# Listing an expert layer's tokens in one burst of bf16 products, and adding up a paired expert earlier

## The chip, the cores and the metric

The kernel runs on one core of one Trainium2 chip. The metric is device microseconds of one execution, from the first to the last instruction of the program with what lies around them. A core has a matrix engine (TensorE, PE in the profile, with its weight loads shown apart as PEld), a vector engine (VectorE, DVE), a scalar engine (ScalarE, ACT), a general engine (GpSimd, POOL) and a queue engine that here only issues transfers (SyncE, SP). Weights come from HBM over 16 DMA engines.

## The reference, cut to what matters

Two transformer layers over 256 tokens of width 1024. The second layer ends in a mixture of experts: each token goes to 2 of 8 experts, and this part reads most of the bytes, since every expert has three matrices of 1024 x 3584 float32 (44 MB).

```python
logits = (xf @ router).astype(jnp.float32)
top_v, top_i = lax.top_k(logits, TOP_K)
gates = jax.nn.softmax(top_v, axis=-1)
dense_g = jnp.sum(jax.nn.one_hot(top_i, N_EXPERTS) * gates[..., None], axis=1)
y = jnp.zeros_like(xf)
for e in range(N_EXPERTS):
    y = y + dense_g[:, e:e + 1] * swiglu(xf, wg[e], wu[e], wd[e])
# swiglu(x, wg, wu, wd) = (silu(x @ wg) * (x @ wu)) @ wd
```

All inputs and the output are float32. After it comes a residual layer norm.

## The kernel before, in words

The attention parts and the dense channel mixer of the first layer take the first third of the time; the change does not touch them. `Route` finds, for each token and expert, whether the token is chosen (`maskf`), its place in the expert's list (`pos`) and its weight (`gate`). `Route.ones` issues small products whose results nobody uses, between the two halves of the router's products.

The experts run in the order `ORDER = [1, 0, 2, 4, 5, 6, 7, 3]`; below, position 0 is expert 1, and so on. Each is entered through a `tc.Switch` on the number of its tokens, with one arm for each of six sizes (`CLASSES`). In the profiled data position 0 and position 4 take the same arm, `(64, 0)`: up to 64 tokens, two column groups of the array side by side. Positions 1 and 2 (`HEAVY` and `LIGHT`) run as a pair, group by group in turns, in `both()`: the heavy one has up to 128 tokens in split precision (three products each, from parts `wh` and `wl` that ScalarE and VectorE write) and a second part of 32 tokens ("beyond"); the light one has 32.

An expert's columns are cut into two chunks, c = 0 (2048 columns) and c = 1 (1536). Its stages are: gate products (m = 0) and up products (m = 1) for c = 0, the same for c = 1, then the down products for both chunks. Weights move in pieces of 1 MB (42 to an expert) through 18 buffers (`halves`). `done(u)` issues the transfer of the piece 18 places later on SP's queue as soon as a piece has been used. So TensorE can be up to 18 pieces behind the transfers, and the transfers stop where all 18 are full.

Tokens of an expert are fetched by `gather`: GpSimd clears `x_sb` and issues an indirect transfer from the rows `x_rows` in HBM, at the row numbers `slot_row`. They are then transposed on TensorE and copied (`pick`), into `xg`. `bring` adds an expert's result to the sum `acc`: four products with a one-hot matrix, then four VectorE additions.

`list_tokens` makes `slot_row`. For each of eight experts VectorE writes a one-hot matrix of 2 x 256 columns in float32 (L978), into halves of one tile, so that two experts fit at a time; TensorE multiplies it with the token numbers in four products of one column each (L981); at the end VectorE turns the sums into row numbers (L982, L983). A float32 product is two weight loads and two matmuls in the trace. The call stands ahead of the c = 1 chunk of position 0:

```python
if i == 0 and c == cs[-1]:
    list_tokens()
    gather(HEAVY, 0)
    gather(LIGHT, 0, 32, 1)
```

At the end of the pair, `bring_light` (`before_end`) is called after the heavy expert's last group of down products. Then the "beyond" part is added up (`scatter_few`, L1193 and L1196, over two "tr" and two "mm" banks of PSUM), the next expert's tokens are picked through two "mm" banks (one copy on VectorE, one on ScalarE, L1184), and the heavy expert is brought in (L1010, L1014). PSUM has 8 banks here: four "acc", two "mm" and two "tr".

The code gives an order, from which a planner makes each engine's instruction list ahead of the run. It may move an instruction forward into a gap that it foresees. [...]

Of the kernel before, what the change touches and what calls it, by code (L numbers as in the profile page):

```python
# [194 lines left out]
def body(ctx, nc, tc, a, out, n_experts=E):  # L195
# [39 lines left out]
    with tc.tile_pool(name="split", bufs=4, side="right") as sp, \  # L235
# [580 lines left out]
        for t in range(2):  # L816
            route.logits(t, ps_tr, ps_mm, x_sb, ident)
            route.choose(t)
            if t == 0:
                route.ones(ps_acc, 20)  # L820
        route.places(ps_tr)
        route.both(ORDER[HEAVY], ORDER[LIGHT])
        gate.close()
# [5 lines left out]
def moe(ctx, nc, tc, a, out, raws, x_sb, hd, route, ident, neghalf, psums, dram, n_experts):  # L829
# [31 lines left out]
    def abreast(m, c):  # L861
        return 4 if m < 2 and c == 0 else 2
# [93 lines left out]
    def whole(tag, n=1024, pool_=wk):  # L956
        return pool_.tile([P, n], F32, name=tag)
# [9 lines left out]
    slot_row = mc.tile([P, 2 * E], I32, name="slot_row")  # L967
    NONE = 2.0 * S

    def list_tokens():  # L970

        tok = whole("wh", pool_=sp)
        pool.iota(tok[:, :2], pattern=[[P, 2]], base=-int(NONE), channel_multiplier=1, allow_small_or_imprecise_dtypes=True)
        ohs, tp = whole("wh", pool_=sp), bank("tr")
        for i, e in enumerate(ORDER[:n_experts]):
            o = ohs[:, i % 2 * 2 * S:(i % 2 + 1) * 2 * S].rearrange("p (t n) -> p t n", t=2)
            for t in range(2):
                dve.tensor_scalar(o[:, t], iota, pos[:, t, e:e + 1], route.maskf[:, t, e:e + 1], op0=ALU.is_equal, op1=ALU.mult)  # L978
            for h in range(2):
                for t in range(2):  # L980
                    pe.matmul(tp[:, 2 * i + h:2 * i + h + 1], o[:, t, h * P:(h + 1) * P], tok[:, t:t + 1], start=t == 0, stop=t == 1)  # L981
        dve.tensor_scalar(slot_token, tp[:, :2 * E], NONE, None, op0=ALU.add)  # L982
        dve.tensor_copy(slot_row, slot_token)  # L983

    def gather(i, h, n=P, to=None):
# [195 lines left out]
    def pick(q, kind="tr"):  # L1181

        tp = picked(x_sb, oh, 4 * q) if kind == "tr" else gathered(0, P, 4 * q, 4, kind)
        (act.copy if q else dve.tensor_copy)(xg[:, q * 512:(q + 1) * 512], tp)  # L1184

    def scatter_few(sc, y):

# [17 lines left out]
    def expert(i, cls, mine, sc2, after=None, before_end=None, mate=None):  # L1205
        e, ws = ORDER[i], widths(i)
        final = i + 1 == n_experts
        parts = [mate] if mate else [Part(xg, *p_) for p_ in CLASSES[cls]]
        paired = mate or before_end
        grouped = final and parts[0].n == 32  # L1210
# [17 lines left out]
        turn = parts[:]  # L1228
        cs = ds = range(len(ws))

        def by_turns(units, n, f, between=None):

            for u0 in range(0, len(units), n):
                yield
                for p_ in turn:
                    if p_ in to_pick:
                        to_pick.remove(p_)
                        pick_beyond(p_)
                    for u in units[u0:u0 + n]:
                        f(p_, u)  # L1240
                turn.reverse()
                for u in units[u0:u0 + n]:
                    done(u)
                if between:
                    between(u0 + n)

        def down(c):
            units = units_of(i, c, 2)

            def between(n):  # L1250

                if c == ds[-2]:
                    for p_ in parts:
                        p_.turned(ws[-1], {1: {4: (0, 1), 6: (2,)}, 2: {4: (0,), 6: (1,)}, 4: {6: (0,)}}[p_.g].get(n, ()))


            narrow = {1: 4, 3: 1, 5: 3}.get(cls, 0)
            yield from by_turns(units, abreast(2, c) if paired else len(parts), lambda p_, u: p_.down(
                u, c == 0 and u[3] == 0, c == ds[-1] and u == units[-1],
                256 if c == ds[-1] and u[3] < narrow and not p_.off else 512), between)  # L1260

        for c in cs:
            width = ws[c]
            if i == 0 and c == cs[-1]:
                list_tokens()
                gather(HEAVY, 0)
                gather(LIGHT, 0, 32, 1)
            if beyond and c == cs[-1]:
                shares(sc2, e, P, beyond[0].n)
            for m in range(2):  # L1270

                n = abreast(m, c) if paired else 4 if few and c < cs[-1] else len(parts)
                units = units_of(i, c, m)
                turn[:] = parts if len(units) // n % 2 else parts[::-1]
                if m == 0 and c == cs[0]:
                    turn[:] = parts
                yield from by_turns(units, n, lambda p_, u: p_.products(m, u))
                if m == 0 and c > cs[0] and not at_once:
                    for p_ in parts:
                        p_.turned(ws[c - 1])  # L1280
                for p_ in turn[::-1]:
                    p_.active(m, width)
            if at_once and c < cs[-1]:
                for p_ in parts:
                    p_.turned(width)
# [20 lines left out]
        turn[:] = parts[::-1]  # L1306
        if before_end:
            gather(i + 2, 0)
        yield from down(len(ws) - 1)
        if before_end:  # L1310
            before_end()
        for p_ in beyond:
            if few and not final:
                act.copy(p_.h[0][:, :S], p_.y[0][:, :S])
# [115 lines left out]
    for i, e in enumerate(ORDER):  # L1430
        if i == LIGHT:
            continue
        if i == 0:
            onehot(oh, e, 0, route.maskf)
            for q in range(2):
                pick(q)
            for t in range(2):
                act.activation(acc[:, t], x_sb[:, t], AF.Copy, scale=ALPHA)
            arms[HEAVY] = (nc.values_load(route.pair[0:1, 0:1], min_val=0, max_val=len(HEAVY_ARMS) - 1), len(HEAVY_ARMS))
        else:  # L1440
            for q in range(2):
                pick(q, "mm")
            bring(sc, ORDER[i - 2 if i - 1 == LIGHT else i - 1])
            if i != HEAVY and i + 1 < n_experts:
                gather(i + 1, 0)
        for cls in tc.Switch(*arms[i], f"expert{i}"):
            if i != HEAVY:
                run(expert(i, cls, sc, sc2, i + 1))
            elif cls:
                both()  # L1450
            else:

                gather(LIGHT, 0)
                flow, usual = laid(False), (flow, place)
                place = {u: q for q, u in enumerate(flow)}
                for q in range(len(halves)):
                    fetch(pair_start + q)
                for q in range(2):
                    pick(q, "mm")
                gather(HEAVY, 0)  # L1460
                for kind in tc.Switch(kinds[ORDER[LIGHT]], len(CLASSES), "light"):
                    run(expert(LIGHT, kind, sc, sc2))
                for q in range(2):
                    pick(q, "mm")
                bring(sc, ORDER[LIGHT])
                gather(LIGHT + 1, 0)
                for kind in tc.Switch(kinds[ORDER[HEAVY]], len(CLASSES), "heavy"):
                    run(expert(HEAVY, kind, sc, sc2, LIGHT + 1))
                flow, place = usual
# [14 lines left out]
```

## Time and profile before

| what | value |
|---|---|
| runs | 1330.01 us median of 3 (1320.58 to 1333.2) |
| profiled execution | 1327.82 us, of which 1326.0 us from the first to the last instruction |
| mean granted TensorE clock | 0.97 |
| TensorE busy | 1267.2 us (96%) |
| VectorE, ScalarE, GpSimd busy | 459.3, 360.9, 45.3 us |
| moved from HBM | 427.73 MB |

The profile is of one execution. Times of a row are in microseconds from the span's start, or lengths; a group's mean is in nanoseconds. "idle before <-X" names what the engine waited for. A matmul's length in a row includes the time that its result takes to come out, so in a row of many the union of all, not the sum, is the time spent. "PEclk" is the share of full clock that TensorE was granted.

### The profile page before, as it was taken

What the parts mean: (1) busy time and instruction counts of PE and PEld (TensorE: products, weight loads), DVE (VectorE), ACT (ScalarE), POOL (GpSimd) and SP (SyncE); (2) the same over time, 40 slices, a digit from 0 to 9 for tenths busy, and PEclk for the clock granted to TensorE, in tenths of its full rate; (3) what the DMA queues carried; (4) which work ended last, traced back from release to release, by engine and by line L of the source; (5) the groups of instructions that cost most, each with busy time, mean ns of one, the idle gap of its engine ahead of it and who ended that gap; (6) DMA issues with size and microseconds to landing.
All of it is one profiled execution on the core that took longest, in us unless ns stands there. A gap on an engine that the chain in (4) does not pass through costs nothing.

```text
span 1326.0 us, 21614 instructions
## 1 busy us (share of the span) xinstructions
PE 1267.2 (96%) x8971; PEld 777.5 (59%) x8971; DVE 459.3 (35%) x742; ACT 360.9 (27%) x638; POOL 45.3 (3%) x64
## 2 busy tenths in 40 slices
PE   9999999999998799999999999999999999999974
PEld 8978999998987454545665642443542443243331
DVE  4689455567677210336544440001010001000102
ACT  4584444453573100244543410000000000000001
POOL 1010000000001000000000000000000000000000
PEclk9999999999999889999999999999999999999985
DMA  9537455553627899989999979998999999999895
GB/s 331 203 96 258 187 190 182 178 205 136 219 96 302 312 417 406 395 363 410 408 420 418 420 297 377 361 367 330 415 418 415 413 419 415 388 420 412 337 417 241
DMA packets 98026, 430.60 MB, mean 325 GB/s; under 512 B 10403, under 2 KB 16547, under 8 KB 67244
## 3 DMA queue, kind: packets, MB, share of 16 engines
q1 hardware_dynamic: 95804, 422.75, 80.9%
q0 software_dynamic: 2032, 5.63, 1.3%
q8 instruction: 81, 1.33, 0.4%
q14 instruction: 109, 0.89, 0.2%
HBM read 427.73 MB, written 2.11 MB: 324 GB/s over the span
## 4 chain that ended last, share of the span: by engine, by line
PE 82%; DMA 6%; issue 2%; DVE 2%; ACT 1%; POOL 0%; SPq 0%; DVEq 0%; ACTq 0%; POOLq 0%
PE acc L1090 15%; PE acc L1153 15%; PE mm L1090 14%; PE mm L344 4%; PE mm L343 4%; PE mm L345 4%; PE acc L1023 3%; PE acc L345 3%; PE acc L1025 3%; PE acc L344 3%; PE acc L343 3%; PE acc L1024 3%; DMA piece<-in_moe_w_down_dram 3%; PE tr L1123 2%; DMA piece<-in_moe_w_up_dram 1%
## 5 line engine op out<-in xcount | busy, mean ns | idle before, releaser
L1090 PE MATMUL acc<-piece,xg 128*64 128x512 f32 (+5 forms) x1488 | 191.9, 502 | 0.0
L1153 PE MATMUL acc<-piece,hT 128*32 128x256 f32 (+2 forms) x1504 | 175.2, 459 | 8.9 <-DMA piece<-in_moe_w_down_dram 8.9
L307 DVE TENSOR_TENSOR wl<-piece,wh 128x1024 fp32r<-128x1024 f32 (+4 forms) x124 | 135.0, 1098 | 87.9 <-ACT wh L305 85.1
L1090 PE MATMUL mm<-piece,xg 128*64 128x512 f32 (+5 forms) x896 | 143.2, 528 | 15.1 <-issue 5.5
L305 ACT ACTIVATE wh<-piece 128x1024 fp32r<-128x1024 f32 (+4 forms) x124 | 118.1, 958 | 81.6 <-PE acc L344 40.6
L1090 PEld LDWEIGHTS acc<-piece,xg 128*32 128x32 f32 (+1 forms) x1488 | 71.4, 120 | 114.6 <-issue 101.1
L1153 PEld LDWEIGHTS acc<-piece,hT 128*32 128x32 f32 (+1 forms) x1504 | 71.0, 123 | 104.2 <-issue 72.2
L343 PE MATMUL mm<-xTh,wl 128*128 128x256 f32 x448 | 126.7, 283 | 0.0
L344 PE MATMUL mm<-xTh,wh 128*128 128x256 f32 x448 | 126.5, 282 | 0.0
L345 PE MATMUL mm<-xTl,wh 128*128 128x256 f32 x448 | 126.4, 282 | 0.0
L1104 DVE TENSOR_TENSOR hd<-hd,acc 128x512 f32<-128x512 f32 (+1 forms) x24 | 14.5, 630 | 298.7 <-PE acc L1090 297.2
L838 DVE TENSOR_TENSOR wl<-piece,wh 128x1024 fp32r<-128x1024 f32 (+1 forms) x80 | 88.1, 1117 | 76.2 <-PE acc L1025 51.0
L1090 PEld LDWEIGHTS mm<-piece,xg 128*64 128x64 f32 (+1 forms) x896 | 56.9, 131 | 96.2 <-issue 84.7
L1111 ACT ACTIVATE hT<-tr 128x512 f32<-128x512 f32 (+2 forms) x30 | 15.6, 542 | 327.9 <-PE tr L1123 315.2
L837 ACT ACTIVATE wh<-piece 128x1024 fp32r<-128x1024 f32 (+1 forms) x80 | 75.8, 973 | 68.8 <-PE acc L1024 68.6
L343 PEld LDWEIGHTS mm<-xTh,wl 128*128 128x128 f32 x448 | 85.0, 190 | 0.2
L344 PEld LDWEIGHTS mm<-xTh,wh 128*128 128x128 f32 x448 | 84.2, 188 | 0.2
L345 PEld LDWEIGHTS mm<-xTl,wh 128*128 128x128 f32 x448 | 84.2, 188 | 0.0
L1169 DVE COPY hd<-acc 32x256 f32<-32x256 f32 (+2 forms) x12 | 6.6, 554 | 163.4 <-ACT hd L1169 107.5
L343 PE MATMUL acc<-wh,xTl 128*128 128x512 f32 (+2 forms) x128 | 46.7, 365 | 0.0
L345 PE MATMUL acc<-wl,xTh 128*128 128x512 f32 (+2 forms) x128 | 46.3, 363 | 0.0
L344 PE MATMUL acc<-wh,xTh 128*128 128x512 f32 (+2 forms) x128 | 46.2, 361 | 0.0
(474 smaller groups left out, 1648.2 us busy)
## 6 DMA issues: line engine op xcount, KB each, us to landing
piece<-in_moe_w_down_dram SPq DMA_DIRECT2D x95, 1024.0 KB, 15.5
piece<-in_moe_w_gate_dram SPq DMA_DIRECT2D x60, 1024.0 KB, 14.1
piece<-in_moe_w_up_dram SPq DMA_DIRECT2D x58, 1024.0 KB, 16.2
piece<-in_moe_w_up_dram SPq DMA_DIRECT2D x30, 768.0 KB, 10.2
piece<-in_moe_w_gate_dram SPq DMA_DIRECT2D x29, 768.0 KB, 8.5
piece<-in_moe_w_up_dram SPq DMA_DIRECT2D x28, 512.0 KB, 10.1
piece<-in_moe_w_gate_dram SPq DMA_DIRECT2D x26, 512.0 KB, 9.5
piece<-in_ffn_w_gate_dram SPq DMA_DIRECT2D x5, 2048.0 KB, 7.8
```

Of the source, the lines that this page charges most:

```text
L305: hi = act.activation(h, src, AF.Copy)
L307: return hi, dve.tensor_sub(lo, src, h.bitcast(F32))
L343: pe.matmul(ps, lt[1], rt[0], start=start, stop=False)
L344: pe.matmul(ps, lt[0], rt[0], start=False, stop=False)
L345: pe.matmul(ps, lt[0], rt[1], start=False, stop=stop)
L837: act.activation(h, src, AF.Copy)
L838: dve.tensor_sub(lo, src, h.bitcast(F32))
L1023: pe.matmul(ps, lt[1], rt[0], start=start, stop=False)
L1024: pe.matmul(ps, lt[0], rt[0], start=False, stop=False)
L1025: return pe.matmul(ps, lt[0], rt[1], start=False, stop=stop)
L1090: pe.matmul(self.ps[b][q * self.n:(q + 1) * self.n, c0:c0 + (jb - ja) * w], self.tokens(k), block[:, ja - j0:jb - j0, cols], **at)
L1153: latest["down"] = pe.matmul(y[g * self.n:(g + 1) * self.n, c + q:c + q + b], self.hidden(u, j), v[:, j, i * w + q:i * w + q + b], **at)
```

## The change

The one-hots of all eight experts are written in bf16 into one tile (`marks`) when position 0 starts. `list_tokens` runs ahead of the up products of chunk c = 0, one stage earlier than before, as 32 products in a row, each of two columns (token number, and a one that marks a filled place). The two gathers move with it. `bring_light` is called amid the heavy expert's last group of down products, after the part that runs first there. The picks behind the pair go through "acc" banks, and both of their copies run on ScalarE. `Route.ones` issues 16 products in place of 20.

```diff
-                route.ones(ps_acc, 20)
+                route.ones(ps_acc, 16)
...
-    def list_tokens():
-
-        tok = whole("wh", pool_=sp)
-        pool.iota(tok[:, :2], pattern=[[P, 2]], base=-int(NONE), channel_multiplier=1, allow_small_or_imprecise_dtypes=True)
-        ohs, tp = whole("wh", pool_=sp), bank("tr")
+    token = sc.bitcast(BF16)[:, :4].rearrange("p (t c) -> p t c", t=2)
+    pool.memset(token, 1.0)
+    pool.iota(token[:, :, 0], pattern=[[P, 2]], base=0, channel_multiplier=1, allow_small_or_imprecise_dtypes=True)
+
+    def mark_tokens():
+
+        marks = whole("hT", 2048).bitcast(BF16).rearrange("p (i t n) -> p i t n", t=2, n=S)
         for i, e in enumerate(ORDER[:n_experts]):
-            o = ohs[:, i % 2 * 2 * S:(i % 2 + 1) * 2 * S].rearrange("p (t n) -> p t n", t=2)
             for t in range(2):
-                dve.tensor_scalar(o[:, t], iota, pos[:, t, e:e + 1], route.maskf[:, t, e:e + 1], op0=ALU.is_equal, op1=ALU.mult)
+                dve.tensor_scalar(marks[:, i, t], iota, pos[:, t, e:e + 1], route.maskf[:, t, e:e + 1], op0=ALU.is_equal, op1=ALU.mult)
+        return marks
+
+    def list_tokens(marks):
+
+        tp = bank("tr")[:, :4 * E].rearrange("p (i h c) -> p i h c", h=2, c=2)
+        for i in range(n_experts):
             for h in range(2):
                 for t in range(2):
-                    pe.matmul(tp[:, 2 * i + h:2 * i + h + 1], o[:, t, h * P:(h + 1) * P], tok[:, t:t + 1], start=t == 0, stop=t == 1)
-        dve.tensor_scalar(slot_token, tp[:, :2 * E], NONE, None, op0=ALU.add)
+                    pe.matmul(tp[:, i, h], marks[:, i, t, h * P:(h + 1) * P], token[:, t], start=t == 0, stop=t == 1)
+        to = slot_token.rearrange("p (i h) -> p i h", h=2)
+        dve.tensor_scalar(to, tp[:, :, :, 1], -NONE, NONE, op0=ALU.mult, op1=ALU.add)
+        dve.tensor_add(to, to, tp[:, :, :, 0])
         dve.tensor_copy(slot_row, slot_token)
...
     def pick(q, kind="tr"):
...
-        (act.copy if q else dve.tensor_copy)(xg[:, q * 512:(q + 1) * 512], tp)
+        (act.copy if q or kind == "acc" else dve.tensor_copy)(xg[:, q * 512:(q + 1) * 512], tp)
...
+        marks = None if i else mark_tokens()
...
-        def by_turns(units, n, f, between=None):
+        def by_turns(units, n, f, between=None, amid=None):
...
                     for u in units[u0:u0 + n]:
                         f(p_, u)
+                    if amid and p_ is turn[0] and u0 + n >= len(units):
+                        amid()
...
-            if i == 0 and c == cs[-1]:
-                list_tokens()
-                gather(HEAVY, 0)
-                gather(LIGHT, 0, 32, 1)
...
             for m in range(2):
+                if marks is not None and c == 0 and m:
+                    list_tokens(marks)
+                    gather(HEAVY, 0)
+                    gather(LIGHT, 0, 32, 1)
...
-        yield from down(len(ws) - 1)
-        if before_end:
-            before_end()
+        yield from down(len(ws) - 1, before_end)
...
-                pick(q, "mm")
+                pick(q, "acc" if i - 1 == LIGHT else "mm")
```

More of the change, by code (lines that the diff above doesn't have):

```diff
@@ L1245, in by_turns, with down @@
                     between(u0 + n)
-        def down(c):
+        def down(c, amid=None):
             units = units_of(i, c, 2)
@@ L1259, in down @@
                 u, c == 0 and u[3] == 0, c == ds[-1] and u == units[-1],
-                256 if c == ds[-1] and u[3] < narrow and not p_.off else 512), between)
+                256 if c == ds[-1] and u[3] < narrow and not p_.off else 512), between, amid)
         for c in cs:
             width = ws[c]
-            if i == 0 and c == cs[-1]:
-                list_tokens()
-                gather(HEAVY, 0)
-                gather(LIGHT, 0, 32, 1)
             if beyond and c == cs[-1]:
```

## The prediction

> **What bounds the kernel now.** I read the page first: the span, the engines' busy time, the slices and the chain.
>
> ```profile
> span 1326.0 us, 21614 instructions
> PE 1267.2 (96%) x8971; PEld 777.5 (59%) x8971; DVE 459.3 (35%) x742; ACT 360.9 (27%) x638; POOL 45.3 (3%) x64
> ...
> PE 82%; DMA 6%; issue 2%; DVE 2%; ACT 1%; POOL 0%; SPq 0%; DVEq 0%; ACTq 0%; POOLq 0%
> ```
>
> TensorE is busy 96% of the span and holds 82% of the chain that ended last. From the page alone, less work for TensorE is less time. But the experts stream 352 MB, so I cut the expert part into stretches (columns: stretch, length, busy time and instructions of five engines, granted clock, DMA share, GB/s), and then asked who waited for weights.
>
> ```profile
> 447.00:565.00 118.00, 114.51 (x569) 57.56 (x570) 22.21 (x42) 15.32 (x24) 5.99 (x7) 0.91 0.95 380
> 565.00:573.00 8.00, 8.00 (x70) 2.21 (x73) 0.05 (x1) 0.00 (x0) 0.00 (x0) 1.00 0.67 250
> 573.00:783.00 210.00, 205.96 (x1556) 123.54 (x1549) 110.00 (x114) 89.76 (x109) 2.93 (x3) 0.99 1.01 413
> 783.00:790.00 7.00, 7.00 (x33) 2.06 (x36) 2.94 (x5) 0.00 (x0) 1.00 (x1) 1.00 0.12 30
> 790.00:910.00 120.00, 117.78 (x941) 46.11 (x934) 6.05 (x11) 7.78 (x16) 2.89 (x3) 1.00 0.96 368
> 910.00:1243.00 333.00, 326.38 (x2385) 133.99 (x2389) 25.41 (x43) 21.21 (x43) 6.73 (x7) 1.00 0.99 402
> 1243.00:1309.00 66.00, 54.06 (x549) 21.76 (x541) 3.23 (x7) 2.45 (x5) 0.00 (x0) 0.81 0.98 396
> ```
>
> ```profile
> PEld acc L1153 <- DMA piece<-in_moe_w_down_dram: 14.4, 10, 2.4
> PE mm L1090 <- DMA piece<-in_moe_w_gate_dram: 2.4, 1, 2.4
> ```
>
> Both are near their limit, but they take turns. TensorE's waits for weights, of which these are the longest, lie behind 1233 us: asked of the stretch from 1233 to 1310 alone, the view gives the same two rows. Until then TensorE sets the pace, and the transfers run up to 18 pieces ahead. In the last 66 us it is reversed: TensorE is busy 54 of them, and the transfers finish what TensorE's progress at 1243 us allowed them to start. **The end therefore moves with TensorE's progress at 1243 us**, as long as the transfers can follow.
>
> Can they? The highest rate over a long stretch is 413 GB/s. What is spare below it: 8 x (1 - 250/413) = 3.2 us, 7 x (1 - 30/413) = 6.5 us, 120 x (1 - 368/413) = 13.1 us; together **22.8 us of spare transfer time from 565 to 910 us**. A TensorE that runs earlier by less than that finds its buffers full again at 910, as now. In between it lives on the 18 buffers: 18 x 1.05 MB at 413 GB/s are 46 us of lead when full.
>
> **The list: what goes.** Rows of the old list's own instructions, and the chain in order of time (start, length, what) around it at position 0, then the same stages of position 4, which takes the same arm.
>
> ```profile
> L981 PE MATMUL tr<-wh x64: 250/250/373, 476.9 to 495.8; 128*128 128x1 f32 x64
> 478.00:497.00 19.00, 19.00 (x91) 11.56 (x93) 4.92 (x15) 0.00 (x0) 0.00 (x0) 0.69 1.02 422
> ...
> 447.71 15.57 PE mm L1090 x64
> ...
> 477.01 1.88 PE tr L981 x16
> ...
> 504.07 1.15 PE tr L1123 x8
> 505.22 10.48 PE acc L1090 x72
> ...
> 910.02 13.95 PE mm L1090 x64
> ...
> 937.71 10.33 PE mm L1090 x72
> 948.04 1.15 PE tr L1123 x8
> 949.19 10.48 PE acc L1090 x72
> ...
> 985.18 0.69 DVE hd L1169
> ```
>
> Position 0 spends 504.07 - 477.01 = 27.06 us on its gate stage with the list inside; position 4 spends 10.33 us on that stage without it. The stages behind agree to the hundredth (1.15, 10.48), so the comparison is fair. **The list costs 27.06 - 10.33 = 16.7 us**, more than its 64 instructions, since the granted clock fell to 0.69 there and slowed the gate products between them too.
>
> **The list: what comes.** 32 bf16 products of two columns. The nearest row is the dummy products of `ones`, also bf16, 128 x 128 weights and few columns.
>
> ```profile
> 424.03 0.51 PEld L133 LDWEIGHTS <-tri 128*128 128x128 bf16 x14
> 424.14 0.49 PE L133 MATMUL acc<-tri 128*128 128x8 bf16 x14
> 481.14 0.97 PEld L981 LDWEIGHTS tr<-wh 128*128 128x128 f32 x8 [0.39 <-issue]
> 448.48 1.38 DVE L978 TENSOR_SCALAR wh<-iota,pos,maskf 128x256 f32<-128x256 bf16 x4 [6.73 <-issue]
> 476.28 0.69 DVE L1104 TENSOR_TENSOR hd<-hd,acc 128x512 f32<-128x512 f32 x1 [26.42 <-PE acc L1090]
> ```
>
> 14 loads in 0.51 us are 36 ns each, so 32 take 1.2 us; with 0.2 for the turn to another weight shape (the eight transposes take 1.15 us in the chain, and eight float32 loads 0.97 below) I take **1.4 us**. The bounds are 32 x 0.036 = 1.2 and, at the float32 load's 0.97/8 = 0.121, 3.9 us. The sum is 16.7 - 1.4 = **15.3 us** (12.8 to 15.5).
>
> [...]
>
> The one-hots move to VectorE's start at position 0. Four took 1.38 us, 16 take 5.5: from 448.5 to 454, and 2.8 us would be the bound below if bf16 output halved them. VectorE then has nothing until 476.28, where it had waited 26 us, and the burst stands at about 463, so the cover is 9 us; were it gone, each microsecond would be one on TensorE. Three VectorE instructions make the row numbers behind the burst, in the same idle time. The tile of the one-hots is the single one in which the expert's transposed columns stand later; these come at 504 now, 489 then, 25 us behind the burst. GpSimd clears `x_sb` at the same point as before, and its two indirect transfers leave some 30 us earlier: 0.6 MB, 1.5 us of a stream with 22.8 to spare. Nothing waits on GpSimd's queue behind them. `token`'s two small instructions stand ahead of all this on an idle GpSimd. Four fewer products in `ones` are 4 x 0.036 = 0.14 us; I count nothing.
>
> **The pair's end.** The timeline there (start, length, engine, line, operation):
>
> ```profile
> 763.12 1.98 PE L1010 MATMUL tr<-x_sb,oh 32*128 32x512 f32 x4 [0.91 <-ACT x_sb L1169]
> 768.71 1.12 PE L1010 MATMUL mm<-x_sb,oh 32*128 32x512 f32 x2
> 770.76 0.30 PEld L1025 LDWEIGHTS acc<-wl,hT 128*128 128x128 f32 x2 [0.41 <-DVE acc L1014]
> 775.59 0.69 PE L1010 MATMUL mm<-x_sb,oh 32*128 32x512 f32 x1
> 776.75 0.75 DVE L1014 SCALAR_TENSOR_TENSOR acc<-mm,gate,acc 128x512 f32<-128x512 f32 x1 [1.05 <-PE mm L1010]
> 777.56 0.18 PEld L1193 LDWEIGHTS mm<-h,sc 32*128 32x128 f32 x1 [0.81 <-DVE acc L1014]
> 777.90 0.79 PE L1193 MATMUL mm<-h,sc 32*128 32x256 f32 x3
> 778.33 1.29 DVE L1196 TENSOR_TENSOR acc<-acc,tr 128x512 f32<-128x512 f32 x2 [0.83 <-PE mm L1193]
> 780.62 1.06 PE L996 MATMUL mm<-ident,x_sb 128*128 128x128 f32 x8 [1.94 <-DVE acc L1196]
> 781.52 1.88 PE L1010 MATMUL tr<-hd,sc 128*128 128x512 f32 x4
> 785.05 3.65 PE L1090 MATMUL mm<-piece,xg 128*64 128x512 f32 x16
> ```
>
> The planner had already pulled three of the light expert's four products forward (two instructions each, from 763.12 and 768.71); the last stands at 775.59, behind the group. Amid the group, it no longer makes L1193 wait 0.81 us for its addition. The picks (L996) in "acc" banks no longer wait 1.94 us for "mm". New is that `bring` (L1010) now comes first to the "tr" banks, free after the first two L1196. Then: L1193 ends at 778.69 - 0.81 = 777.9; L1196 starts at 777.5 and has two done at 778.8; the picks end at 777.9 + 1.06 = 778.95 beside that; `bring` starts at about 778.95 where it started at 781.52. **2.6 us** less, of which I take 2.5. The two copies on ScalarE, one behind the other, lie under `bring`'s 3.5 us of products (781.52 to 785.05); without that cover the second would cost 0.7, the length of L1104 on the same shape. The added wait: VectorE's two additions of 0.75 stand ahead of the group's last splits, which L1025 needs; it already waits at 770.76. If both delay the splits, the gain is 2.6 - 1.5 = 1.1, and it is lost if the planner puts them worse still; 0 to 2.75 are the bounds.
>
> **The sum.** 15.3 + 2.5 = 17.8 us off, below the 22.8 that the transfers can follow. Against the profiled execution's 1327.8 us this gives 1310.0. The median of before, 1330.0, lies 2.2 above it, so I move up by half of that and forecast **1311 us**. A difference of under 1% (13 us) is about what a measurement of this kernel can't tell from no change.
>
> **Rivals.**
> - *The burst is dear, or the planner scatters it.* As one dear burst (3.9 us): 1314. Scattered among products of the experts, one turn for each expert as in the old list: eight turns of 0.2 into the other shape and 0.2 out of it, and 3.9 of loads, are 7.1 us; the gain is 9.6 + 2.5 and the time 1317. For it: the old list was scattered. Against: the old one had to wait for VectorE's next pair of one-hots, the new one has all by 454 us. [...]
> - *The transfers are the bound.* If the lead in the pair is smaller than the 46 us suggest, TensorE waits there and only 3.2 + 6.5 us of spare are usable before 790: 1318. For it: 1.01 of DMA share from 573 to 783. Against: no wait for weights of TensorE there, and 7 idle us at its end.
> - *The change doesn't do what it says*, since the planner, given another program, orders the pair's 240 us otherwise. Three in a hundred of that (7 us) either way: 1304 or 1318.
> - *Slower.* Position 4 uses 44 MB from 910 to 985 us, 75 us, while 413 GB/s bring 31 MB; with 18.9 MB in full buffers 5.9 MB are left, 14 us of transfer. If TensorE's earlier start finds the stream over 14 us short of full, TensorE waits piece by piece as behind 1243 us, where the granted clock is 0.81: 75/0.81 is 18 us more, and some 6 of waiting, 1311 + 24 = 1335. It decides only where the 22.8 us of spare prove smaller than 4, so I hold it unlikely.
>
> **How the numbers follow.** Forecast 0.62 (1305 to 1316); dear or scattered burst 0.12; transfers 0.07; another order 0.07 slower and 0.07 faster; slower 0.05. The range of 8 in 10 takes the forecast with the runs' own spread of several us, the dear burst and half of the cases at 1318, and leaves out the slower case and the best orders: 1301 to 1321. Faster by over 1%: the forecast, the quicker order and some of the dear burst, 0.75; within 1%: 0.21; slower: 0.04.
>
> **What would show it.** In the changed profile: 32 bf16 products of the list in one row of 1 to 2 us behind the first stage (447.7 + 15.6); the gate stage behind in 10.3 us without a dip of the clock; position 1 some 15 us earlier; L996 with no wait for L1196; position 3 some 18 us earlier; under 3 us idle transfers about 565 us, and buffers full again by 910 less 18. Wrong it would be by waits for weights before 1200 us, by a pair that is longer than 236 us, or by a clock below 0.9 behind the burst.

## The result and the profile after

The changed kernel takes **1320.5 us** (median of 20 executions, 1313.9 to 1325.0) where the kernel before took 1328.1 on the same chips: a ratio of **0.994, interval 0.993 to 0.996**, 7.6 us less where 1311 us, some 17 less than those 1328, was forecast. The profiled execution took 1324.1 us. Its lines stand some nine further down: L1090 is now L1099, L1153 L1162, L981 L988, L996 L1005, L1010 L1019, L1014 L1023, L1023 to L1025 L1032 to L1034, L1193 L1202, L1196 L1205, L1169 L1178, and the switch at L1480 stands at L1490.

The page of the changed kernel: span, TensorE's row, shares of the chain.

```profile
span 1322.3 us, 21535 instructions
PE 1256.1 (95%) x8935; PEld 768.1 (58%) x8935; DVE 457.7 (35%) x742; ACT 361.9 (27%) x639; POOL 45.4 (3%) x65
PE 79%; DMA 8%; issue 3%; DVE 2%; ACT 1%; POOL 0%; SPq 0%; DVEq 0%; ACTq 0%; POOLq 0%
```

TensorE's busy time fell by 11.1 us (1267.2 before), the span by 3.7. "issue", time in which the chain waits for nothing that the profile shows, rose from 2% to 3%. The chain of the changed kernel in order of time, position 0 (start, length, what):

```profile
447.38 16.80 PE mm L1099 x64
464.18 0.89 PE tr L988 x32
465.07 13.88 PE acc L1099 x64
478.95 10.33 PE mm L1099 x72
489.28 1.16 PE tr L1132 x8
490.44 10.48 PE acc L1099 x72
...
526.44 0.69 DVE hd L1178
...
536.03 1.06 issue
537.09 1.03 PE tr L1005 x8
538.12 8.96 PE acc L1077 x16
```

The list is one row of 0.89 us behind the first stage, and the gate stage takes 10.33 us, as at position 4. Position 0 ends at 526.4 where it ended at 541.2: **14.8 us** are gained by then. At the pair's first gate product (538.1, 549.4 before) 11.3 are left, at the first product behind the pair (779.7, 785.05 before) 5.3. So 3.5 us go on the way into the pair, and 5.9 in the pair, nearly all at its end. The way in, TensorE's timeline of the changed kernel (in brackets the idle time ahead of the row, and what ended it):

```profile
529.45 1.88 PE L1019 MATMUL acc<-hd,sc 128*128 128x512 f32 x4
537.09 1.03 PE L1005 MATMUL tr<-ident,x_sb 32*128 32x32 f32 x8 [5.76 <-issue]
```

TensorE stands still for 5.76 us, and the view names no engine or transfer that releases it. What it did is seen when the trace is asked for the line of the switch: TensorE's two jumps there, behind position 0 and into the pair (count, then shortest, median and longest in ns, and the first and last start). First the changed kernel, then the kernel before:

```profile
L1490 PEldq COMPARE_BRANCH  x2: 329/3194/6058, 523.0 to 530.8; - x2
```

```profile
L1480 PEldq COMPARE_BRANCH  x2: 328/368/408, 537.8 to 543.7; - x2
```

**The jump into the pair took 6.06 us; before it took 0.41.** It begins at 530.8 and ends at 536.8, just ahead of the first transposes. The data were there before: the kernel list_join below has its jump over at 529.4, and its sequencer then waits until 534.05 for VectorE's first addition of position 0's result (L1023), which ends at 534.00; in the kernel before, that wait ended at 548.68 and the addition at 548.64. In the changed kernel that addition ends at 534.04, and the same wait, behind the late jump, takes 0.05 us. So about 3.0 of the 5.76 us are due to the jump.

The end of the pair in the changed kernel, in order of time (rows of the timeline, then three stretches with the granted clock, the third number from the end):

```profile
752.04 2.34 PE L1019 MATMUL tr<-x_sb,oh 32*128 32x512 f32 x4 [0.91 <-ACT x_sb L1178]
754.31 1.93 PE L1162 MATMUL acc<-half,hT 128*32 128x256 f32 x16
756.18 3.78 PE L1019 MATMUL mm<-x_sb,oh 32*128 32x512 f32 x4
759.88 1.94 PE L1162 MATMUL acc<-last,hT 128*32 128x256 f32 x16
761.75 0.80 PE L1032 MATMUL acc<-wh,hTl 128*128 128x512 f32 x1
...
769.77 1.28 DVE L1205 TENSOR_TENSOR acc<-acc,tr 128x512 f32<-128x512 f32 x2 [1.07 <-PE mm L1202]
770.98 1.28 DVE L1205 TENSOR_TENSOR acc<-acc,mm 128x512 f32<-128x512 f32 x2
773.59 1.55 PE L1005 MATMUL acc<-ident,x_sb 128*128 128x128 f32 x8 [3.83 <-issue]
774.93 3.12 PE L1019 MATMUL tr<-hd,sc 128*128 128x512 f32 x4
```

```profile
752.00:764.00 12.00, 11.96 (x46) 4.77 (x47) 5.69 (x7) 3.59 (x5) 0.00 (x0) 0.57 1.01 423
764.00:768.00 4.00, 4.00 (x18) 3.04 (x17) 2.36 (x2) 1.06 (x1) 0.00 (x0) 1.00 1.02 423
774.00:778.00 4.00, 4.00 (x11) 2.23 (x10) 0.75 (x1) 1.17 (x2) 1.95 (x2) 0.57 0.35 131
```

Four things are to be seen. All four of the light expert's products (L1019, two instructions each) now stand ahead of the group's full products (L1032). The clock is at 0.57 over the 12 us in which these products of 32 rows or 32 columns run: 3.78 us for four instructions that take 1.98 at full clock. TensorE no longer waits in the midst of L1202, as forecast. But it then stands still for 3.83 us ahead of the picks, again with "issue" as the only cause, and it comes back to a clock of 0.57.

The jumps of the changed kernel at that place (line of the switch, 755 to 795 us), and of the kernel before:

```profile
L1490 PEldq COMPARE_BRANCH  x2: 2151/3087/4023, 769.2 to 774.6; - x2
```

```profile
L1480 PEldq COMPARE_BRANCH  x2: 1592/1888/2185, 778.2 to 781.8; - x2
```

Here is the row that the prediction misread: before, TensorE's first jump behind the pair started at 778.17 and took 2.19 us, so it ended at 780.36, a quarter of a microsecond ahead of the picks at 780.62. The view put their 1.94 us of idle down to VectorE's addition, the third of which had ended at 780.22. Behind the jump, the sequencer's waits for other engines took 0.05 us each, so what they wait for was done. In all thirteen kernels below that keep this jump long, the picks begin 0.27 to 0.45 us after it ends.

What a late jump waits for: the queue rows of the page count code that is brought in by transfers, here 16.3 KB a packet,

```profile
q8 instruction: 82, 1.34, 0.4%
```

and in the trace the packet that starts at 534.28 us and takes 1.08 is landed 1.5 us before the jump of 6.06 us ends; it started 3.5 us after the jump did. That this queue brings TensorE's code is read from such times alone: in each of the 18 late jumps of the table below (5 into the pair, 13 behind it) a packet of it lands 1.4 to 1.6 us before the jump ends. From 559.8 to 743.5 us, where TensorE has no jump, 12 packets start, and in the 11 intervals between them it runs 1423 products and 1416 weight loads: 258 for each packet.

### The profile page after: what moved, and what is told of

It reads as the page before. It is cut to its first block, busy times and chain, and to the rows that moved or that the text cites. A ratio compares the mean times of both kernels' runs of the same rounds, so it can differ in the third digit from the quotient of the medians.

```text
span 1322.3 us, 21535 instructions
## 1 busy us (share of the span) xinstructions
PE 1256.1 (95%) x8935; PEld 768.1 (58%) x8935; DVE 457.7 (35%) x742; ACT 361.9 (27%) x639; POOL 45.4 (3%) x65
## 3 DMA queue, kind: packets, MB, share of 16 engines
HBM read 427.73 MB, written 2.11 MB: 325 GB/s over the span
## 4 chain that ended last, share of the span: by engine, by line
PE 79%; DMA 8%; issue 3%; DVE 2%; ACT 1%; POOL 0%; SPq 0%; DVEq 0%; ACTq 0%; POOLq 0%
PE acc L1099 15%; PE mm L1099 14%; PE acc L1162 13%; DMA piece<-in_moe_w_down_dram 4%; PE mm L344 4%; PE mm L343 4%; PE mm L345 4%; PE acc L1032 3%; PE acc L345 3%; PE acc L1034 3%; PE acc L344 3%; PE acc L343 3%; PE acc L1033 3%; DMA piece<-in_moe_w_gate_dram 2%; DMA piece<-in_moe_w_up_dram 2%
## 5 line engine op out<-in xcount | busy, mean ns | idle before, releaser
L1099 PE MATMUL acc<-piece,xg 128*64 128x512 f32 (+5 forms) x1488 | 192.1, 502 | 0.0
L1162 PE MATMUL acc<-piece,hT 128*32 128x256 f32 (+2 forms) x1504 | 173.4, 453 | 9.5 <-DMA piece<-in_moe_w_down_dram 9.5
L1099 PE MATMUL mm<-piece,xg 128*64 128x512 f32 (+5 forms) x896 | 141.0, 521 | 17.1 <-issue 8.6
L1099 PEld LDWEIGHTS acc<-piece,xg 128*32 128x32 f32 (+1 forms) x1488 | 71.2, 120 | 114.2 <-issue 97.8
L1162 PEld LDWEIGHTS acc<-piece,hT 128*32 128x32 f32 (+1 forms) x1504 | 70.5, 122 | 103.9 <-issue 71.5
L1099 PEld LDWEIGHTS mm<-piece,xg 128*64 128x64 f32 (+1 forms) x896 | 55.1, 129 | 101.3 <-issue 85.2
L1178 DVE COPY hd<-acc 32x256 f32<-32x256 f32 (+2 forms) x12 | 6.7, 554 | 163.5 <-ACT hd L1178 107.5
```

What stands on the lines that cost most here:

```text
L1099: pe.matmul(self.ps[b][q * self.n:(q + 1) * self.n, c0:c0 + (jb - ja) * w], self.tokens(k), block[:, ja - j0:jb - j0, cols], **at)
L1162: latest["down"] = pe.matmul(y[g * self.n:(g + 1) * self.n, c + q:c + q + b], self.hidden(u, j), v[:, j, i * w + q:i * w + q + b], **at)
```

## The experiments

"End of the pair" is the stretch from the light expert's first scattered product to the next expert's first product; "jump in" is TensorE's jump into the pair, "jump behind" its first jump behind it. All from one profile of each kernel; ratios are to the kernel before, on the same chip, from 20 executions of the whole change and 4 to 10 of each other. An interval is some 3 us to either side, so a difference of 2 to 4 us between two rows is mostly not clear of noise by the times; there the profiles carry the argument.

| kernel | jump in, us | jump behind, us | end of the pair, us | ratio (95%) |
|---|---|---|---|---|
| before | 0.41 | 2.19 | 21.9 | 1 |
| whole change | 6.06 | 4.02 | 27.7 | 0.994 (0.993 to 0.996) |
| again | 6.10 | 6.06 | 24.7 | 0.995 (0.993 to 0.997) |
| list_alone | 5.96 | 2.30 | 23.3 | 0.993 (0.991 to 0.995) |
| end_alone | 0.41 | 4.30 | 27.9 | 1.002 (0.999 to 1.004) |
| moved_edge | 5.94 | 0.33 | 24.3 | 0.995 (0.993 to 0.997) |
| list_join | 0.30 | 2.32 | 23.2 | 0.989 (0.987 to 0.992) |
| list_join_again | 0.31 | 2.25 | 23.1 | 0.989 (0.986 to 0.991) |
| list_arm | 0.41 | 3.02 | 28.4 | 0.989 (0.986 to 0.993) |
| list_join_edge | 0.40 | 0.43 | 24.6 | 0.990 (0.988 to 0.993) |
| full_rows | 5.97 | 4.08 | 23.7 | 0.992 (0.990 to 0.995) |
| all_join | 0.31 | 6.22 | 31.0 | 0.994 (0.992 to 0.997) |
| list_join_rows | 0.51 | 2.77 | 23.4 | 0.988 (0.985 to 0.991) |
| all_join_edge_rows | 0.41 | 0.44 | 21.3 | 0.988 (0.985 to 0.991) |
| amid_only | 0.41 | 4.17 | 27.7 | 0.992 (0.989 to 0.995) |
| picks_only | 0.43 | 2.46 | 23.3 | 0.992 (0.989 to 0.994) |
| all_join_edge | 0.41 | 0.31 | 25.6 | 0.991 (0.988 to 0.994) |

**again**, the changed kernel once more:

> The changed kernel as it is, once more. In its first profile TensorE stood still for 5.8 us with nothing to wait for but its own next instructions ('issue') ahead of the pair's first transposes (537 us), and for 3.8 us ahead of the next expert's picks behind the pair (773.6 us). Theory A (code comes late: the place of the program's blocks of instructions decides): both stand again, 5.8 and 3.8 us, in any execution. Theory B (an accident of one execution): one or both are gone, below 2 us, and this execution is some 4 us shorter. Time against the kernel before: 0.994 (-7.6 us) either way.

Both stand again: 5.75 us of idle ahead of the pair, 5.86 ahead of the picks. The late code is no accident of one execution. The clock stayed at 1.0 up to that idle time, so the products were through 4.8 us earlier; 2.0 of these went into a longer wait for the code.

**list_alone** takes the end's three edits back:

```diff
-        yield from down(len(ws) - 1, before_end)
+        yield from down(len(ws) - 1)
+        if before_end:
+            before_end()
...
-        (act.copy if q or kind == "acc" else dve.tensor_copy)(...)
+        (act.copy if q else dve.tensor_copy)(...)
...
-                pick(q, "acc" if i - 1 == LIGHT else "mm")
+                pick(q, "mm")
```

> Only the list in one burst, with the one-hots written beforehand; the pair's end and the picks are those of the kernel before. Theory 1 (the pair's new end costs some 5.7 us, and the list brings its 14.8 us): the stretch from the light expert's first scattered product to the next expert's first product is back at 22 us, and the time is 11 to 14 us below the kernel before (1314 to 1317), lower than with the whole change. Theory 2 (the forecast's step on the pair's end is right, and the list's gain is lost elsewhere, in the transfers or at the jumps): 2.5 us above the whole change, so some 5 us below the kernel before (1323).

**end_alone** keeps these and has the old list of the kernel before:

> Only the light expert's addition amid the last group and the copies on ScalarE; the list stays as it was in the kernel before. Theory 1 (the four products of 32 rows, drawn ahead of the group's full products, lengthen the half clock there, and the removed waits lay beneath the fetching of code): the stretch from the light expert's first scattered product to the next expert's first product takes 26 to 28 us instead of 22, and the time is 2 to 5 us above the kernel before. Theory 2 (the forecast): that stretch takes 19.5 us and the time is 2.5 us below the kernel before.

The list alone is 0.993, 9.7 us below the kernel before by the ratio (11.7 by the medians, where 11 to 14 were expected). The end alone is at 1.002, on the side of a loss that its interval doesn't show, and its end of the pair is 27.9 us in place of 21.9. Both agree with theory 1, and by the ratios the two parts add up to the whole (-9.7 + 2.1 = -7.6).

The 21.9 us of the kernel before are in part luck. Behind the picks the clock falls to half for some us in fifteen of the seventeen profiles (0.50 from 769 to 773 us in list_alone, behind 2.09 us of idle), and from the picks to the next expert it takes 6.0 to 7.4 us; in the kernel before and in moved_edge it stayed full there, and that took 4.4 and 4.5.

**moved_edge** makes TensorE's code of the pair 120 instructions longer at its start:

```diff
+        idle = bank("mm")
+        for _ in range(60):
+            pe.matmul(idle[:, :8], iota[:, :P], iota[:, :8], start=True, stop=True)
         act.activation(x, gathered(1, 32, 0, KD, "tr"), AF.Copy)
```

> The whole change, and 60 bf16 products of 8 columns, used by nobody, ahead of the pair's first transposes. They make TensorE's part of the pair 120 instructions longer, so that the edge of a block of 256 instructions, which now lies 28 instructions ahead of the pair's end, lies some 150 ahead of it. They cost 60 x 0.03 = 1.8 us at the pair's start at most, nothing where TensorE waits there anyway. Theory 1 (the picks behind the pair wait for the block of code that is asked for at that edge, some 6 us before): the 3.8 us of idle ahead of the picks fall below 1.5 us, the clock is not halved behind them, and the stretch from the light expert's first scattered product to the next expert's first product shrinks from 27.7 to 22 to 24 us; in all 2 to 4 us below the whole change. Theory 2 (TensorE waits there for its data, or for the jump itself, wherever the edge lies): the 3.8 us stay, and the time is up to 1.8 us above the whole change.

The block of 256 agrees with the 258 instructions to a packet above; the 28 and the 150 ahead of the pair's end are an estimate, which no view shows. The jump behind the pair fell to 0.33 us. It is 0.31 to 0.44 in all four kernels with these 60 products, and 2.2 to 6.2 in all thirteen without. But the idle ahead of the picks fell only to 2.1 us (moved_edge's jumps, and the row of its picks):

```profile
L1493 PEldq COMPARE_BRANCH  x2: 325/1192/2060, 771.4 to 775.5; - x2
774.10 1.16 PE L1005 MATMUL acc<-ident,x_sb 128*128 128x128 f32 x8 [2.11 <-DVE acc L1205]
```

Now the view names VectorE's additions (L1205) rightly: the jump was over at 771.75, and the picks begin 0.20 us after the third of the four additions, as they do in the two other kernels with these picks and the 60 products. So the picks in the acc banks wait for these additions too; why, no run shows. The end of the pair was 24.3 us, with a half clock ahead of the idle time, 3.3 less than in the whole change. The 60 products cost 1.7 of these (the way into the pair takes 13.3 us, 11.6 in the whole change). By the times nothing is left (0.995); where the rest goes is not shown.

**list_join** is list_alone with no change to any instruction that is executed. It lengthens an arm of position 0's switch that these inputs never take, the last in the program:

```diff
         marks = None if i else mark_tokens()
+        if i == 0 and cls == 5:
+            idle = bank("mm")
+            for _ in range(32):
+                pe.matmul(idle[:, :8], iota[:, :P], iota[:, :8], start=True, stop=True)
```

> The list alone, and 32 products in an arm of position 0 that is never taken here (its last one in the program). What TensorE executes is the same to the instruction; only the place of the code behind that switch, as far as it follows from the arm in front of it, is as in the kernel before (1727 instructions in the last arm instead of 1664; 1729 before). In all kernels with the burst TensorE's jump into the pair took 5.9 to 6.1 us, in both kernels with the old list 0.4. Theory A (the place of the code behind the switch decides whether the pair's code is there in time): the jump takes 0.4 us, the stretch from position 0's end to the pair's first gate product shrinks from 11.2 us to 8.1 to 9, and the time falls 2.5 to 3 us below the list alone: some 1313 against 1327 before. Theory B (the length of the executed arm, 940 instead of 1004 instructions, decides): the jump keeps its 6 us, and the time is that of the list alone.

TensorE's jumps of list_join at that place, and the row of its timeline ahead of which the changed kernel stood still:

```profile
L1496 PEldq COMPARE_BRANCH  x2: 301/317/333, 523.1 to 529.1; - x2
```

```profile
534.10 0.68 PE L1005 MATMUL tr<-ident,x_sb 32*128 32x32 f32 x8 [2.67 <-issue]
```

The jump in takes 0.30 us, the way into the pair 8.2 us (11.2 in list_alone), and the ratio is 0.989. **list_join_again**, with five executions in place of four, gives 0.989 too, 15.3 us below the kernel before:

> The list alone with the 32 products in the arm that is never taken, once more, with more executions: 0.989 if its lead is real, 0.992 if it was an accident of the few executions. Jump into the pair 0.3 to 0.4 us again.

So the place of the code alone is worth some 3 us here by the profiles. By the times it is 2 to 6, by medians or ratios, and the intervals overlap. **list_arm** has the same 32 products in the executed arm (`cls == 1`) instead:

> The list alone, and the same 32 products in the executed arm of position 0, at its start: it is 1002 instructions long, as in the kernel before (1004), instead of 940; the last arm keeps 1664. They cost about 1 us (0.03 each). Theory A (the place of the code behind the switch): the jump into the pair still takes 6 us and the time is 1 us above the list alone. Theory B (the executed arm's length): the jump takes 0.4 us, the stretch from position 0's end to the pair's first gate product is 8.1 to 9 us, and the time is some 2 us below the list alone.

The jump was 0.41 us, so theory A as I had put it, by the last arm's length, falls; but the two kernels differ in nothing that could tell the theories apart, since a longer arm anywhere ahead moves the code behind the switch by the same 62 or 63 instructions. What is shown is that moving it by so much decides. By what rule a place is good or bad stays open. The end of the pair, 28.4 us with the old order, shows one more thing: the clock was at 0.50 from 755 to 763 us there, a dip as long as that of the whole change.

**list_join_edge**, list_join with the 60 products of moved_edge:

> The list alone, the 32 products in the arm that is never taken, and the 60 unused products of 8 columns at the pair's start that moved the edge of TensorE's code there. If theory A holds (place of the code) and the edge does at the old end of the pair what it did at the new one: jump into the pair 0.4 us, with the 60 products (1.8 us) lying beneath the wait for the gathered rows there; jump behind the pair 0.4 us instead of 2.3 to 6; idle ahead of the picks 2 us (the additions of the scattered rows, which are waited for now). The stretch behind the pair stays at 21 to 23 us, and the time is 3 to 4 us below the list alone, the lowest so far: 1312. If the waits for data there are as long as those for code: the same as the list with the other place of code alone, or up to 1.8 us above it.

The jump behind the pair falls to 0.43 us here too, and nothing is gained (0.990). The picks stand still for 2.2 us there, which the view puts down to VectorE's additions, where those of list_join stood still for 2.1 until the jump was over; and the 60 products lengthen the way into the pair from 8.2 to 9.5 us.

**full_rows** lets the light expert's four products run over all 128 rows:

```diff
-            bring(hot[:32], ORDER[LIGHT], y, ("tr", "mm"))
+            bring(hot, ORDER[LIGHT], whole_y, ("tr", "mm"))
```

> The whole change, with the light expert's four scattered products over all 128 rows instead of 32 (the rows beyond have one-hots of zero; the same columns stream, so the same time at full clock). In three of the four profiles with the new end the clock was at 0.5 for 10 us from the first of these products on, in one it was at 1.0 throughout; with the old end it was at 0.5 for 3.5 us in one and never in the other. Theory 1 (products of few rows hold the clock down): the clock stays at 1.0 in this stretch, first scattered product to last product of the group's rest 12.9 us instead of 17.7, and the median of the times is 2 to 3 us below the whole change. Theory 2 (narrow products of 32 columns hold it down, or the power of the whole core): the dip appears as often as before, 17.7 us, and the time is that of the whole change (0.994 to 0.995).

At full clock four of these instructions take 1.98 us with 32 rows (L1010 at 763.12 us in the kernel before) and 1.98 with 128 (L1019 in all_join_edge_rows below).

**list_join_rows**, the same edit on list_join:

> The same, and the light expert's four scattered products over 128 rows instead of 32 (one-hots of zero in the rest). With 32 rows the clock dipped to 0.5 at the end of the pair in six of nine profiles, for 1 to 10 us; with 128 rows in none of one. Theory 1 (few rows hold the clock down): no dip, end of the pair 23 us, and the time is 0 to 3 us below the kernel without this edit (0.987 to 0.989). Theory 2 (chance): a dip comes two times in three, and the time is the same.

No dip ahead of the picks in any of the three kernels with 128 rows; with 32 rows there is one in six of seven profiles with the new end and in three of seven with the old. Theory 1 agrees with that, but it is not shown: if the rows made no difference, three given profiles of these seventeen would all be among the eight without a dip one time in twelve. That the new order brings the dip more often rests on the same few profiles. By the times the edit is worth 3 us at most with the new end, which is not clear of noise, and nothing that can be told with the old.

**all_join**, the whole change with the 32 products of list_join:

> The whole change, and the 32 products in the arm of position 0 that is never taken, which put the code behind that switch where the pair's jump took 0.3 us. Theory A (the list brings 15 us, the place of that code took 3 of them back, and the new end of the pair costs 2 to 5): the jump into the pair takes 0.4 us, the stretch from position 0's end to the pair's first gate product 8 to 9 us instead of 11.6, the end of the pair stays at 24.7 to 27.7, and the ratio to the kernel before falls from 0.994 to 0.991 or 0.992. Theory B (what is saved at the jump is waited for later, in the transfers): 0.994 as without them.

Theory A fails by the time: the jump in is 0.31 us, but the ratio stays at 0.994. Its profile shows where the 3 us may have gone: an end of the pair of 31.0 us (jump behind 6.22, half clock), and one more late jump, into position 5, 5.97 us where the kernel before took 0.98. The next two take that end apart.

**amid_only**, list_join with the addition amid the last group and nothing else of the end:

> The list with its code in place (as list_join), and of the pair's end only the light expert's addition amid the last group; the picks stay in the banks of the kernel before, with one copy on VectorE. Theory 1 (drawing the four products of 32 rows together, ahead of the group's rest, is what costs: a half clock of up to 10 us in most executions, and then the group's 16 products so close before the jump that the code for the picks comes 4 to 6 us late): end of the pair 25 to 31 us against 23.2 without it, 2 to 5 us above list_join, 0.991 to 0.993. Theory 2 (the picks in other banks cost): 23 us, 0.989 as list_join.

```profile
748.59 1.98 PE L1019 MATMUL tr<-x_sb,oh 32*128 32x512 f32 x4 [0.91 <-ACT x_sb L1178]
750.50 1.81 PE L1162 MATMUL acc<-half,hT 128*32 128x256 f32 x16
752.23 3.77 PE L1019 MATMUL mm<-x_sb,oh 32*128 32x512 f32 x4
755.94 1.93 PE L1162 MATMUL acc<-last,hT 128*32 128x256 f32 x16
...
770.03 1.06 PE L1005 MATMUL mm<-ident,x_sb 128*128 128x128 f32 x8 [3.87 <-issue]
```

The timeline has the two marks of the whole change, 3.77 us for the thin products and 3.87 us of idle: end of the pair 27.7 us, and 0.992 against 0.989, with overlapping intervals. **picks_only**:

> The list with its code in place, and of the pair's end only the next expert's picks in the acc banks, both copies on ScalarE. Theory 1: the picks wait for VectorE's additions of the scattered rows as before (2 us of idle ahead of them), end of the pair 22 to 24 us, and the time is that of list_join, 0.989. Theory 2: end of the pair 25 us or more, 0.991 to 0.994; the jump from position 4 to position 5, which took 6 us in all_join alone, may be long again, since this edit moves the code behind it by one instruction.

The end of the pair is that of list_join (23.3 us), and yet the ratio is 0.992. TensorE's jumps between positions 4 and 5 in picks_only show a likely cause:

```profile
L1496 PEldq COMPARE_BRANCH  x2: 330/3281/6232, 968.0 to 974.4; - x2
```

The edit makes the code behind the pair one instruction longer, and the jump into position 5 takes 6.23 us, as in all_join, 0.9 to 1.1 in list_join and amid_only. TensorE stands still for 4.80 us ahead of that position's first product, 2.17 in list_join. **all_join_edge** and **all_join_edge_rows** repair the whole change:

> The whole change with the code behind position 0 in place and the edge of TensorE's code moved, but the light expert's four products over 32 rows as in the change. Theory 1 (the edge takes the late code away, and the dip of the clock stays): first jump behind the pair 0.4 us, idle ahead of the picks 2.1 us, a dip in three or four executions of five, end of the pair 24 us with it and 20 without, 0.989 to 0.991. Theory 2 (the dip goes with the late code): no dip, end of the pair 20 us, 0.988 as with 128 rows.

> The whole change with all three repairs: the place of the code behind position 0, the edge of TensorE's code 150 instructions ahead of the pair's end (60 unused products), 128 rows in the light expert's four products. If each does what its own run showed: jump into the pair 0.4 us, no dip at the pair's end (12.9 us up to the last product of the group's rest), 2.1 us of idle ahead of the picks and 4.5 us from there to the next expert, 19.5 us in all against 23.2 of the list alone, at 1.3 us for the 60 products: 2 us below the list alone with its code in place, so 0.987 to 0.988. If the edits don't add up: 0.990 to 0.992.

```profile
751.11 1.98 PE L1019 MATMUL tr<-x_sb,oh 128*128 128x512 f32 x4 [0.91 <-ACT x_sb L1178]
753.02 1.07 PE L1162 MATMUL acc<-half,hT 128*32 128x256 f32 x16
754.02 1.98 PE L1019 MATMUL mm<-x_sb,oh 128*128 128x512 f32 x4
755.94 1.07 PE L1162 MATMUL acc<-last,hT 128*32 128x256 f32 x16
...
766.12 1.17 PE L1005 MATMUL acc<-ident,x_sb 128*128 128x128 f32 x8 [2.11 <-DVE acc L1205]
```

This is the timeline of all_join_edge_rows: the same four rows in 5.8 us where they took 9.7 in the whole change, and the idle ahead of the picks ended by data. The clock over this stretch:

```profile
751.00:764.00 13.00, 12.89 (x80) 7.20 (x80) 8.56 (x10) 5.29 (x8) 0.00 (x0) 1.00 1.01 418
```

In all_join_edge the jump behind the pair took 0.31 us and the dip stayed (products of the light expert at half clock, as in moved_edge), so the dip doesn't come from the late code. From all_join on, the 60 products take 5.3 us off the end of the pair (31.0 to 25.6) and the rows another 4.4 (to 21.3), one profile each. The time, 0.988, is that of the list alone with its code in place: with these losses repaired, the new end wins nothing that can be told.

## Why the prediction was right and where it was wrong

- **The list: right.** Forecast 15.3 us, measured 14.8 at the end of position 0. The burst took 0.89 us where 1.4 was taken: by the trace 28 ns for each product, below the 36 of the dummy products, so the dear burst falls. The 16 one-hots took VectorE 4.19 us, neither the 5.5 of the forecast nor the halved 2.8. The first stage gave 1.2 us back (16.80 against 15.57, with a clock of 0.81 from 447 to 463 us in place of 0.89).
- **The transfers: right.** list_join and list_join_again end 14 to 15 us below the kernel before, so the whole of the list's gain reaches the end once it isn't lost on the way; TensorE's products had no long waits for weights ahead of 1225 us (none in list_join, one of 2.0 us in the changed kernel). The slower rival did not come.
- **The pair's end, -2.5 us: wrong in sign.** It cost 4 to 6 us in most profiles (1.4 from list_alone to again, 7.7 from list_join to all_join) and about 2 to 4 in the times. The failed step is "The picks (L996) in "acc" banks no longer wait 1.94 us for "mm"". They waited for code: the jump ended 0.27 us before them. Under it lies a wait for VectorE's additions, which the other banks don't remove (2.11 us in moved_edge). The step "Amid the group, it no longer makes L1193 wait 0.81 us" held, but the 0.81 us were a wait of the weight loads; TensorE's products stood still for 0.41. And the order that does it was costed at nothing: it sets 8 products of 32 rows and 32 of 32 columns in one row, where the old order put full products in between, and the clock is at half for up to 10 us in six of seven profiles. That the order causes this is likely and not shown. The lower bound of this term stood at nothing gained, with no reason given against a loss.
- **Missing from the sum: where the code lies.** Neither the forecast nor a rival has TensorE's jump into the pair, 0.41 us before and 6 us in every kernel with a list of 64 instructions fewer in each arm and nothing to make up for them. Some 3 us of those 5.6 reach the pair's first product, since TensorE waited about 2.6 us there anyway, for VectorE's addition. The rival "orders the pair's 240 us otherwise" had 1318 for a change that doesn't do what it says; the pair's body in fact kept its order and length (214.0 us against 213.8).
- Of the list of signs, five came: the burst (0.89 us, a little under the 1 to 2), the gate stage, position 1 about 15 us earlier as far as its switch (14.8), no wait of L1005 for L1205 in the view (though for a reason that the view doesn't show), and no idle transfers about 565 us (a DMA share of 1.00 to 1.03 from 550 to 580). At its first product position 1 was 11.3 us earlier, and position 3 was 5 us earlier and not 18. Of the signs of being wrong, one came: a pair longer than 236 us (241.6). Long waits for weights and a low clock behind the burst did not come (it was 1.00 from 463 to 489 us). The difference of 0.6% is clear of no change with 20 executions of each, though the prediction held 1% for too little to tell.

The sum as measured: list 15 off; by the profiles about 3 back at the jump into the pair and about 4 at its end; 7.6 us are left.

One more loss of the profiled execution, ahead of position 4, in a row of its timeline:

```profile
905.91 15.65 PE L1099 MATMUL mm<-piece,xg 128*64 128x512 f32 x64 [3.18 <-issue]
```

Before, the same stage stood behind 1.99 us of idle and took 13.95. With 3.18 us of idle it starts at a clock of 0.64 (906 to 910 us) and takes 1.7 us longer. In the sixteen other profiles the idle time there was 1.4 to 2.9 us, and the stage took 13.95 to 14.05. So 1.2 us more of idle went with almost three of loss, in this one profile.

## What to carry to other kernels

A wait that ends at the same moment as a jump of the same engine may be a wait for code: ask the trace for the line of the switch and read the jumps' durations before you cost the wait's removal at its length. Count the instructions that an edit removes in every arm of a switch, taken or not: code behind it moves, and a jump of 0.4 us can become one of 6; unused products in an arm that is never taken showed here, at no cost, whether that is so. And thin products (few rows or columns) are worth watching: a stretch of them ran at half clock in 9 of 14 profiles, and ran at full clock in all three in which the ones of 32 rows had 128. That is a hint to try, not yet a rule.

## What was not expected of the hardware

- TensorE's jump into the pair took 0.3 to 0.5 us or 5.9 to 6.1 us. The place of the code alone makes that difference for the same executed instructions (5.96 in list_alone, 0.30 in list_join). Behind the pair, where the code was asked for too late, anything from 2.2 to 6.2 us.
- The clock was halved in stretches without idle time, behind 0.91 us of idle that stands there with and without the dip: with products of 32 rows in 9 of 14 profiles, with 128 rows in 0 of 3. In the whole change TensorE was busy for 11.96 of 12 us at 0.57.
- 32 bf16 products of two columns with new weights each took 0.89 us, 28 ns each, though each load of weights is recorded with 95 ns.
